# One PSUM ring for small products and staging, five result banks, and an earlier split of v

## The chip, the cores and the metric

The kernel runs on one core of a Trainium2 chip. The metric is the device time of one execution in microseconds. The engines are TensorE (PE: products; PEld: weight loads), VectorE (DVE), ScalarE (ACT), GpSimd (POOL), and SyncE (SP), which issues most of the transfers.

## The reference

One layer of a streaming encoder, 1024 positions by 1024 channels, in float32:

```
proj = x @ w_in + b_in                      # 4096 columns: u, h, c, b, gate_a, gate_b
y_a  = s5_ssm(u)                            # 32 groups of 16 channels, 64 complex states each
g    = gelu(y_a);  y_a = (g * sigmoid(g @ glu_w + glu_b)) @ w_ssm_out
z    = causal_conv3(c * h);  y_b = (b * z) @ w_conv_out      # v = b * z
x    = LayerNorm(alpha * x + (sigmoid(gate_a) * y_a + sigmoid(gate_b) * y_b) @ w_o)
x    = LayerNorm(alpha * x + (silu(x @ w_gate) * (x @ w_up)) @ w_down)
```

## The kernel before, in words

Every float32 operand of a large product is split into a high half (fp32r) and a low half, and each product is made of three: low by high, high by low, high by high (lines 183 to 185). The input projection and the feed-forward products work on pairs of column blocks with a scheme of seven products in place of eight (`Pair`, ORD_A): each of the seven steps of a pair forms a sum of weight blocks on POOL (`do_add`), splits it on ACT and DVE (`do_split`), and makes twelve products into one of the pair's four PSUM banks. The epilogues (`ev`) copy banks to SBUF on ACT, add them on POOL and DVE, and apply bias, sigmoid or convolution.

PSUM has eight banks of 2 KB in each partition, and one tile of 128 by 512 floats fills a bank. A pool is opened for a stage with `psum_open`: result banks have the tag "mm", n of them. In `psplit` a split stages its high half in PSUM (tag "hp"): ACT copies the raw block to the staging tile (line 137) and to the weights (line 138), and DVE subtracts the staging tile from the raw block (line 115), which frees the staging tile. The convolution stages in such tiles too (`conv`). The SSM branch makes four groups of small products for each of its eight chunks of channels: the transposes pst, the kernel pk, the states psw, the outputs psy, each of 128 by 512 floats at most. These take tiles of the tag "sm" (`small`). Within a tag, a tile takes the buffer that was allotted longest ago and waits for that buffer's last reader. From step 21 of the projection on, the pool psA has four banks for results, two for staging and two for small products.

All engines execute in order. The order is written out by a loop, `run`: at step s it issues the sum for step s+4 (POOL), the split for step s+3 (ACT, DVE), then one piece of each background generator (`bg`: the branch's `mats`, `rot`, `flow`, `gelu`, the convolution), then the twelve products of step s (PE), then epilogues that were put off by one step (`flush`), then the copies of step s. So a small product stands on PE ahead of the products of the step at which its generator is advanced. `begin_b` stands behind the last step of the projection (`steps[n_co - 1].mid`): it splits v into vh and vl, eight tiles, which the first products with w_conv_out (`pso`, the next steps) read. `begin_glu` closes psA.

Of the kernel before, what the change touches and what calls it, by code (L numbers as in the profile page):

```python
# [9 lines left out]
F32 = mybir.dt.float32  # L10
# [5 lines left out]
P = 128  # L16
# [31 lines left out]
def kernel(  # L48
# [29 lines left out]
    def opened(name, side="left", **kw):  # L78
        cm = pool(name, side, **kw)
        return cm, cm.__enter__()  # L80

    def close(cm):
        cm.__exit__(None, None, None)
# [33 lines left out]
    def ts(o, a, s1, s2, op0, op1, eng=V):  # L117
        eng.tensor_scalar(o, a, s1, s2, op0, op1)  # L118
# [7 lines left out]

    def staging(dt=F32):
        psum_state["k"] += 1
        return psum_state["p"].tile([P, 512], dt, tag="hp", name=f"hp{psum_state['k']}", bufs=2)

    def psplit(hi, lo, raw):
        if not psum_state["hp"]:
            return split(hi, lo, raw)
        hp = staging(F32R)
        if len(raw.shape) == 3:
            hp = hp.rearrange("p (a b) -> p a b", a=raw.shape[1])
        S.activation(hp, raw, AF.Copy)  # L137
        S.activation(hi, raw, AF.Copy)  # L138
        sub(lo, raw, hp.bitcast(F32))

    psum_state = {"k": 0, "hp": False}

    def psum_open(nm, n=8, hp=False):
        if "cm" in psum_state:
            close(psum_state["cm"])
        psum_state["cm"], psum_state["p"] = opened(nm, space=PSUM)
        psum_state["n"], psum_state["hp"] = n, hp

    def bank(nm):
        return psum_state["p"].tile([P, 512], F32, tag="mm", name=nm, bufs=psum_state["n"])  # L150
# [10 lines left out]
    class Step:  # L161
        load = add = split = mm = None

        def __init__(self):
            self.pre = []
            self.mid = []
            self.after = []

    class Entry:
        def __init__(self, nm):  # L170
# [132 lines left out]
    steps = []  # L303
# [15 lines left out]
    bg = []  # L319

    def flush():
        todo, later[:] = later[:], []
        for f in todo:
            f()

    def run(lo, hi):
        for s in range(lo, hi):
            for f in steps[s].pre:
                f()
            if s + 4 < len(steps) and steps[s + 4].add:  # L330
                steps[s + 4].add()
            if s + 3 < len(steps) and steps[s + 3].split:
                steps[s + 3].split()
            for it in list(bg):
                if it[1] <= s:
                    try:
                        it[1] = s + max(1, next(it[0]) or 1)
                    except StopIteration:
                        bg.remove(it)
            steps[s].mm()  # L340
            flush()
            for f in steps[s].mid + steps[s].after:
                f()
# [40 lines left out]
    def conv(p):  # L384
        q, z, cv = p.f, p.z, p.hs
        zf = z.rearrange("p b k -> p (b k)")
        V.memset(z[:, 0:2, 0:1], 0.0)
        V.tensor_copy(z[:, 0:2, 1:P], z[:, 8:10, 0:127])
        for h in range(2):
            hp = staging()  # L390
            o = 512 * h
            S.activation(hp, zf[:, 256 + o : 768 + o], AF.Copy, scale=cws[:, q, 2:3])
            V.scalar_tensor_tensor(hp, zf[:, 128 + o : 640 + o], cws[:, q, 1:2], hp, ALU.mult, ALU.add)
            V.scalar_tensor_tensor(cv[:, half(h)], zf[:, o : 512 + o], cws[:, q, 0:1], hp, ALU.mult, ALU.add)
            yield 1
        zt[q] = cv
# [36 lines left out]
    def make_x():  # L433
        waiting = []

        def low(h, l, k, src):
            (psplit if k % 2 else split)(h[:, k], l[:, k], src)

        for n, m in enumerate((4, 3, 1, 6, 7, 5, 2)):
            op = XOP[m]  # L440
            if len(op) == 3:
                sums = xcp.tile([P, 4, 512], F32, tag=("xh2", "xl2")[n % 2], name=f"xs{m}")
            h = xh[m] = xcp.tile([P, 4, 512], F32R, tag=f"xh{m}", name=f"xh{m}")
            l = xl[m] = xcp.tile([P, 4, 512], F32R, tag=f"xl{m}", name=f"xl{m}")
            for k in range(4):
                if len(op) == 1:
                    src = xr[op[0]][:, k]
                else:
                    src = sums[:, k]
                    tt(src, xr[op[1]][:, k], xr[op[2]][:, k], OPS[op[0]], G)  # L450
                waiting.append((h, l, k, src))
                if len(waiting) > 2:
                    low(*waiting.pop(0))
                yield 1
        for w in waiting:
            low(*w)
            yield 1
# [40 lines left out]
    def setup():  # L498
# [13 lines left out]
        def carve(*shape, at=None):  # L512
            n = int(np.prod(shape))
            o = used[0] if at is None else at
            if at is None:
                used[0] += n
            t = scr[:, o : o + n]
            return t.rearrange("p (a b) -> p a b", a=shape[0]) if len(shape) == 2 else t
# [10 lines left out]
        dt, a = carve(NG), carve(NG)  # L529
        m, r, q = carve(NG), carve(NG), carve(NG)  # L530
        th, hh, hl = carve(NG), carve(NG), carve(NG)
        it = carve(NG).bitcast(I32)
# [101 lines left out]
        for j in range(8):  # L634
            V.tensor_scalar_mul(sMim[:, :, j], x8[:, :, 7 - j], sgn[:, 0:1])
        ts(nLre, nLre, sgn[:, 0:1], -1.0, ALU.mult, ALU.mult)
        while psum_state["n"] > 4 or next(xg, None):
            yield 1
        close(xst_cm)
        open_ssm()  # L640
# [8 lines left out]
    st = [dict() for _ in range(8)]  # L649

    def small(nm):
        return psum_state["p"].tile([P, 4, P], F32, tag="sm", name=nm, bufs=2)

    def load_bc(cc):
        gs = slice(4 * cc, 4 * cc + 4)
# [4 lines left out]
    def mats(cc):  # L660
# [24 lines left out]
        if cc < 7:  # L685
            load_bc(cc + 1)
        yield 2
        ps = small(f"pst{cc}")
        for g in range(4):
            PE.transpose(ps[:, g, :], B[:, g].rearrange("p j c -> p (j c)"), ident)  # L690
        Bp = s["bp"] = stile([P, 4, P], "bp", f"bp{cc}")
        S.activation(Bp, ps, AF.Copy)
        yield 1
        pk = small(f"pk{cc}")
        for g in range(4):
            PE.matmul(pk[0:16, g, :], B[:, g, 7, :], Cp[:, g, 0:8, :].rearrange("p n c -> p (n c)"),
# [54 lines left out]
    def flow(cc):  # L751
        s = st[cc]
        yield 1
        while cc and "scan" not in st[cc - 1]:
            yield 1
        ps = small(f"psw{cc}")
        for g in range(4):
            PE.matmul(ps[:, g, :], s["bp"][:, g], s["UT"][:, g], start=True, stop=True)
# [217 lines left out]
    def begin_glu():  # L976
        while bg:
            spin()
        close(vst["cm"])
        psum_open("psB")  # L980
        cst_["wcm"], cst_["wp"] = opened("wp", "right")
        cst_["wo"] = []
# [19 lines left out]
    n_co = len(steps)  # L1002
    us = []
    gates = []
    for part in (1, None, 0):
# [8 lines left out]
        for d in range(8):  # L1014
# [3 lines left out]
            if d == 1:  # L1018
                steps.insert(-1, s_.pop(0))
            steps.extend(s_)  # L1020
    steps[n_co - 1].mid.append(begin_b)
    for k in (2, 3):
        steps[n_co - 12 + k].pre.append(lambda k=k: load_v(k))
    steps[n_glu].pre.append(begin_glu)
# [179 lines left out]
    def begin_d():  # L1204
        tr_x1(7, staging)
        close(cst_["tcm"])
        cst_["bcm"], cst_["bp"] = opened("xb")
        for f in make_x1(5):
            f()
# [34 lines left out]
    for f in range(NF):  # L1244
        p = Pair(wgu[0, f], wgu[1, f], f"f{f}", xcombo, epi_f)
# [10 lines left out]
    def begin_d0():  # L1256
        flush()
        psum_open("psD", 6, True)
        close(cst_["wcm"])
        cst_["zcm"], cst_["zp"] = opened("zp", "right")  # L1260
        load_z(0)
# [78 lines left out]


    psum_open("ps0", 6, True)
    pre_cm, pre = opened("pre")
    xst_cm, xst = opened("xst")
    sp = xst

    ramp = tb["ramp"] = pre.tile([P, P], F32, tag="ramp", name="ramp")
    dss = tb["dss"] = pre.tile([16, NG], F32, tag="dss", name="dss")
    early_setup = setup()
    next(early_setup)  # L1350
    raw = pairs[0].raw[1] = wring.tile([P, KT, P], F32, tag="raw", name="raw_u0_1", bufs=4)
# [36 lines left out]
    xg = make_x()  # L1388
# [9 lines left out]
                bg.remove(it)  # L1398

    def small_psum():  # L1400
        psum_open("psA", 4, True)

    steps[21].pre.append(lambda: (flush(), small_psum()))
    run(0, n_x)
    run(n_x, n_end - 1)
    last_after = steps[n_end - 1].after
    steps[n_end - 1].after = []
    run(n_end - 1, n_end)
    steps[n_end - 1].after = last_after

# [285 lines left out]
```

## Time and profile before

| | us |
|---|---|
| three timed runs | 1275.71, 3102.09, 6867.57 |
| their median | 3102.09 |
| the profiled execution | 1276.85 |
| its span, first to last instruction | 1275.1 |

The page gives the busy time of each engine over the span; the table by stretches gives it for any part. Of PE's waits the time-ordered list shows the idle time just before an instruction and what ended it, in square brackets.

### The profile page before, as it was taken

To read this page: it belongs to the slowest core of one execution; us is meant where nothing else is said; L and a number is where in the kernel's file an instruction comes from. 1 tells how busy PE (TensorE), PEld (TensorE's weight loads), DVE (VectorE), ACT (ScalarE), POOL (GpSimd) and SP (SyncE) were. 2 spreads that over 40 slices of the span, in tenths; PEclk is the share of its full clock that TensorE was granted. 3 is DMA by queue.
4 is the path that set the end of the run, shared out by engine and by line. 5 is a ranking of instruction groups with operands and counts; after the bars stand their busy time and mean duration, and the time that the engine had idled before them with its cause. 6 is when DMAs were issued, how large, how long until landed. Compare 5 with 4: busy or idle time off the path is not lost. (4 is left out here: it accounts for less than half of the span.)

```text
span 1275.1 us, 16761 instructions
## 1 busy us (share of the span) xinstructions
PE 1207.8 (95%) x5341; PEld 976.8 (77%) x5341; DVE 836.1 (66%) x1338; ACT 765.7 (60%) x1360; POOL 787.9 (62%) x593
## 2 busy tenths in 40 slices
PE   8769999999899999999979999999999999999996
PEld 4457787787677888888867888888888887888776
DVE  6986887979665656688875444444444447667777
ACT  4675777696876233133664555554555554778891
POOL 5747787797762214323488787777777764544466
PEclk9889999999998999999989999999999999999998
DMA  7122234344446544324303523233223417936312
GB/s 270 59 75 87 85 123 118 112 130 148 138 142 213 194 156 162 116 83 149 132 34 113 181 103 108 93 114 116 100 90 108 156 67 266 370 99 214 101 46 87
DMA packets 88455, 167.63 MB, mean 131 GB/s; under 512 B 17840, under 2 KB 27056, under 8 KB 88112
## 3 DMA queue, kind: packets, MB, share of 16 engines
q1 hardware_dynamic: 87760, 166.44, 39.1%
q8 instruction: 42, 0.69, 0.2%
q14 instruction: 45, 0.37, 0.1%
q10 hardware_dynamic: 608, 0.13, 0.1%
HBM read 116.34 MB, written 44.83 MB: 126 GB/s over the span
## 5 line engine op out<-in xcount | busy, mean ns | idle before, releaser
L183 PE MATMUL ps_f<-x1h,wl_f 128*128 128x512 f32 x616 | 241.7, 392 | 8.7 <-ACT keep L246 3.9
L184 PE MATMUL ps_f<-x1l,wh_f 128*128 128x512 f32 x616 | 240.8, 391 | 0.6 <-DVE x1l L115 0.6
L185 PE MATMUL ps_f<-x1h,wh_f 128*128 128x512 f32 x616 | 240.5, 390 | 0.0
L115 DVE TENSOR_TENSOR wl_f<-t_f,hp 128x512 fp32r<-128x512 f32 x107 | 73.5, 687 | 165.9 <-ACT hp L137 165.7
L137 ACT ACTIVATE hp<-t_f 128x512 fp32r<-128x512 f32 x107 | 64.4, 602 | 164.6 <-POOL t_f L106 158.3
L183 PEld LDWEIGHTS ps_f<-x1h,wl_f 128*128 128x128 f32 x616 | 116.2, 189 | 35.7 <-ACT keep L246 4.3
L184 PEld LDWEIGHTS ps_f<-x1l,wh_f 128*128 128x128 f32 x616 | 116.2, 189 | 24.9 <-DVE x1l L115 1.0
L185 PEld LDWEIGHTS ps_f<-x1h,wh_f 128*128 128x128 f32 x616 | 116.2, 189 | 24.2
L106 POOL TENSOR_TENSOR tB<-B,B 128x512 f32<-128x512 f32 x55 | 71.2, 1294 | 86.1 <-DVE rBl L115 45.4
L1517 PE MATMUL pe<-rBh,rAl 128*128 128x512 f32 x297 | 116.1, 391 | 3.5 <-DVE acc L1507 1.6
L1518 PE MATMUL pe<-rBl,rAh 128*128 128x512 f32 x297 | 115.8, 390 | 1.1 <-DVE rBl L115 1.1
L1519 PE MATMUL pe<-rBh,rAh 128*128 128x512 f32 x297 | 115.6, 389 | 0.0
L183 PE MATMUL ps_gt<-xh,wl_gt 128*128 128x512 f32 x216 | 89.3, 413 | 19.1 <-ACT ec_gt L237 6.2
L185 PE MATMUL ps_gt<-xh,wh_gt 128*128 128x512 f32 x216 | 87.3, 404 | 0.0
L184 PE MATMUL ps_gt<-xl,wh_gt 128*128 128x512 f32 x216 | 86.7, 401 | 0.0
L106 POOL TENSOR_TENSOR t_f<-raw_f,raw_f 128x512 f32<-128x512 f32 x63 | 81.7, 1297 | 2.2 <-DVE wl_f L115 2.0
L1517 PEld LDWEIGHTS pe<-rBh,rAl 128*128 128x128 f32 x297 | 55.7, 188 | 17.1 <-DVE acc L1507 2.5
L183 PEld LDWEIGHTS ps_gt<-xh,wl_gt 128*128 128x128 f32 x216 | 42.1, 195 | 32.0 <-issue 7.1
L138 ACT ACTIVATE wh_f<-t_f 128x512 fp32r<-128x512 f32 x107 | 66.0, 617 | 0.0
L1518 PEld LDWEIGHTS pe<-rBl,rAh 128*128 128x128 f32 x297 | 55.8, 188 | 13.3 <-DVE rBl L115 1.8
L1519 PEld LDWEIGHTS pe<-rBh,rAh 128*128 128x128 f32 x297 | 55.8, 188 | 11.6
L106 POOL TENSOR_TENSOR t_f<-raw_f 128x512 f32<-128x512 f32 x43 | 56.5, 1323 | 10.2 <-DMA raw_f<-in_wgu 9.5
(410 smaller groups left out, 3247.7 us busy)
## 6 DMA issues: line engine op xcount, KB each, us to landing
raw_f<-in_wgu SPq DMA_DIRECT2D x45, 512.0 KB, 4.0
As<-a_d SPq DMA_DIRECT2D x77, 256.0 KB, 3.7
a_d<-hs SPq DMA_DIRECT2D x55, 256.0 KB, 2.0
B<-in_wd SPq DMA_DIRECT2D x44, 256.0 KB, 5.3
s_d<-sg SPq DMA_DIRECT2D x32, 256.0 KB, 2.8
sgd<-s_d SPq DMA_DIRECT2D x16, 512.0 KB, 3.4
raw_gt<-in_w SPq DMA_DIRECT2D x15, 512.0 KB, 4.6
a_d<-hid SPq DMA_DIRECT2D x22, 256.0 KB, 2.1
```

The costliest lines, as they stand in the source:

```text
L106: eng.tensor_tensor(o, a, b, op)
L115: eng.tensor_tensor(o, a, b, ALU.subtract)
L137: S.activation(hp, raw, AF.Copy)
L138: S.activation(hi, raw, AF.Copy)
L183: PE.matmul(ps, self.lo[:, k, :], xh[:, k, :], start=first and k == 0, stop=False, skip_group_check=True)
L184: PE.matmul(ps, self.hi[:, k, :], xl[:, k, :], start=False, stop=False, skip_group_check=True)
L185: PE.matmul(ps, self.hi[:, k, :], xh[:, k, :], start=False, stop=last and k == 3, skip_group_check=True)
L1517: PE.matmul(ps, al[:, c], bh, start=kp == 0, stop=False)
L1518: PE.matmul(ps, ah[:, c], bl, start=False, stop=False)
L1519: PE.matmul(ps, ah[:, c], bh, start=False, stop=kp == NK - 1)
```

## The change

The tag "sm" goes. `small` allots from the tag "hp" like the staging, in a ring of 8 - n buffers; psA is opened with n = 5, so it has five result banks and a ring of three for staging and small products. The pools ps0 and psD have n = 6 and a staging ring of two as before. And `begin_b` is called through a new hook, `next`, directly behind the products of the projection's last step: ahead of the generators' pieces and of the put-off epilogues of that step, which in that one step are issued behind it.

```diff
     def staging(dt=F32):
         psum_state["k"] += 1
-        return psum_state["p"].tile([P, 512], dt, tag="hp", name=f"hp{psum_state['k']}", bufs=2)
+        return psum_state["p"].tile([P, 512], dt, tag="hp", name=f"hp{psum_state['k']}",
+                                    bufs=psum_state["hp"])
...
-        psum_state["n"], psum_state["hp"] = n, hp
+        psum_state["n"], psum_state["hp"] = n, 8 - n if hp else 0
...
+    def advance(s):
+        for it in list(bg):
+            if it[1] <= s:
+                try:
+                    it[1] = s + max(1, next(it[0]) or 1)
+                except StopIteration:
+                    bg.remove(it)
+
     def run(lo, hi):
...
-            for it in list(bg):
-                if it[1] <= s:
-                    try:
-                        it[1] = s + max(1, next(it[0]) or 1)
-                    except StopIteration:
-                        bg.remove(it)
-            steps[s].mm()
+            if steps[s].next:
+                steps[s].mm()
+                steps[s].next()
+                advance(s)
+            else:
+                advance(s)
+                steps[s].mm()
             flush()
...
-        while psum_state["n"] > 4 or next(xg, None):
+        while psum_state["n"] > 5 or next(xg, None):
...
     def small(nm):
-        return psum_state["p"].tile([P, 4, P], F32, tag="sm", name=nm, bufs=2)
+        return psum_state["p"].tile([P, 512], F32, tag="hp", name=nm, bufs=psum_state["hp"]).rearrange(
+            "p (g k) -> p g k", g=4)
...
-    steps[n_co - 1].mid.append(begin_b)
+    steps[n_co - 1].next = begin_b
...
     def small_psum():
-        psum_open("psA", 4, True)
+        psum_open("psA", 5, True)
```

On ACT, at the end of the projection, the order before is this (gy is the gelu, sg the sigmoid of a gate, vh the high half of v):

```order
L121 ACTIVATE wh_so_1_0_3787<-raw_so_1_3679 128x512
L817 ACTIVATE gy_0_3715<-gy_0_3715 128x512
L817 ACTIVATE gy_1_3717<-gy_1_3717 128x512
L407 ACTIVATE sg_0_0_3821<-eb_gt_3704,b1s 128x512
L121 ACTIVATE vh<-vr_z 128x512
L121 ACTIVATE vh<-vr_ws 128x512
```

And this is it with the change (the lines are 10 or 11 higher there):

```order
L121 ACTIVATE wh_so_1_0_3787<-raw_so_1_3679 128x512
L828 ACTIVATE gy_0_3715<-gy_0_3715 128x512
L828 ACTIVATE gy_1_3717<-gy_1_3717 128x512
L121 ACTIVATE vh<-vr_z 128x512
L121 ACTIVATE vh<-vr_ws 128x512
```

The sigmoid moved behind the eight copies of v, and its store on SP with it; the two gelu instructions did not move. On PE, DVE and POOL no instruction changes its place.

Where the ring is used, the order stays, and what changes is which tile has a buffer before which. On ACT, at the branch's first chunk, hp36 to hp39 are staging tiles, bp0 is the copy out of the transposes pst0, K0 the copy out of pk0:

```order
L137 ACTIVATE hp36_920<-t_hc0_6_882 128x512
L138 ACTIVATE wh_hc0_6_918<-t_hc0_6_882 128x512
L137 ACTIVATE hp37_946<-t_hc1_2_916 128x512
L138 ACTIVATE wh_hc1_2_944<-t_hc1_2_916 128x512
L372 ACTIVATE hs0_940<-ps_hc0_1_866,b1s_70 128x512
L137 ACTIVATE hp38_968<-t_hc1_5_942 128x512
L138 ACTIVATE wh_hc1_5_966<-t_hc1_5_942 128x512
L692 ACTIVATE bp0_977<-pst0_972 128x512
L137 ACTIVATE hp39_996<-t_hc1_1_964 128x512
L138 ACTIVATE wh_hc1_1_994<-t_hc1_1_964 128x512
L699 ACTIVATE K0_1005<-pk0_1000 16x512
```

In the ring of three the tiles come as hp36, hp37, hp38, pst0, hp39, pk0: pst0 takes the buffer of hp36 and waits for that split's low half, and pk0 that of hp38.

## Rows read from the trace of the kernel before

**Rows 1.** The page: the span; busy us of an engine, share, instructions.

```profile
span 1275.1 us, 16761 instructions
...
PE 1207.8 (95%) x5341; PEld 976.8 (77%) x5341; DVE 836.1 (66%) x1338; ACT 765.7 (60%) x1360; POOL 787.9 (62%) x593
```

**Rows 2.** Stretches: their length, each engine's busy us, granted clock, DMA share, GB/s.

```profile
99.00:388.00 289.00, 273.94 (x1310) 222.08 (x1309) 224.34 (x315) 216.81 (x368) 222.48 (x159) 0.99 0.41 125
388.00:404.00 16.00, 16.00 (x71) 13.12 (x71) 4.14 (x7) 8.68 (x16) 3.85 (x3) 1.00 0.76 253
404.00:414.00 10.00, 7.06 (x18) 5.01 (x17) 8.36 (x14) 7.86 (x15) 0.00 (x0) 0.66 0.35 103
```

**Rows 3.** PE in order of time: start, us, instruction [idle before <-releaser]; bank waits.

```profile
120.97 0.50 PE L183 MATMUL ps_hc<-xh,wl_hc 128*128 128x512 f32 x1 [0.25 <-DVE ec_hc L112]
...
239.29 0.50 PE L183 MATMUL ps_gt<-xh,wl_gt 128*128 128x512 f32 x1 [2.18 <-DVE ec_hc L112]
...
240.71 0.63 PE L184 MATMUL ps_gt<-xl,wh_gt 128*128 128x512 f32 x1
```

**Rows 4.** ACT and PE in order of time, around the split of v.

```profile
406.35 0.72 ACT L407 ACTIVATE sg<-eb_gt,b1s 128x512 f32<-128x512 f32 x1
406.97 0.61 ACT L121 ACTIVATE vh<-vr_z 128x512 fp32r<-128x512 f32 x1
...
407.64 0.80 PE L183 MATMUL pso<-vh,wl_so 128*128 128x512 f32 x1 [2.94 <-ACT vh L121]
```

**Rows 5.** Waits of ACT, 99 to 388 us: total us, times, longest.

```profile
ACT hp L137 <- DVE zE L387: 4.7, 2, 3.7
...
ACT hp L392 <- DVE hs L394: 1.2, 1, 1.2
...
ACT eb_hc L234 <- PE ps_hc L185: 1.0, 1, 1.0
```

**Rows 6.** PE in order of time, the first, third and last of seven waits.

```profile
309.53 1.03 PE L696 MATMUL pk<-cp,bst 128*16 128x128 f32 x8 [1.53 <-DVE cp L115]
...
336.65 1.03 PE L696 MATMUL pk<-cp,bst 128*16 128x128 f32 x8 [2.48 <-DVE cp L115]
...
372.39 0.50 PE L183 MATMUL ps_gt<-xh,wl_gt 128*128 128x512 f32 x1 [0.86 <-ACT ea_gt L231]
```

**Rows 7.** PE and DVE in order of time: small products, splits ahead in the ring.

```profile
113.41 0.60 PE L690 MATMUL pst<-ident,bst 128*128 128x128 f32 x4
113.73 0.69 DVE L115 TENSOR_TENSOR wl_hc<-t_hc,hp 128x512 fp32r<-128x512 f32 x1 [1.82 <-ACT hp L137]
...
258.15 1.05 PE L758 MATMUL psw<-ut,bp 128*128 128x128 f32 x8
263.29 0.68 DVE L115 TENSOR_TENSOR wl_b<-t_b,hp 128x512 fp32r<-128x512 f32 x1
...
383.51 0.38 PE L789 MATMUL psy<-ut,T 128*128 128x128 f32 x2
383.45 0.68 DVE L115 TENSOR_TENSOR wl_gt<-t_gt,hp 128x512 fp32r<-128x512 f32 x1
```

**Rows 8.** PE and ACT in order of time: last products, the copies of them.

```profile
121.13 0.58 ACT L692 ACTIVATE bp<-pst 128x512 f32<-128x512 f32 x1
...
172.74 0.39 PE L185 MATMUL ps_b<-xh,wh_b 128*128 128x512 f32 x1
174.65 0.58 ACT L234 ACTIVATE eb_b<-ps_b 128x512 f32<-128x512 f32 x1
...
243.50 0.39 PE L185 MATMUL ps_gt<-xh,wh_gt 128*128 128x512 f32 x1
243.93 0.60 ACT L231 ACTIVATE ea_gt<-ps_gt 128x512 f32<-128x512 f32 x1
...
288.84 0.39 PE L185 MATMUL ps_gt<-xh,wh_gt 128*128 128x512 f32 x1
290.04 0.58 ACT L231 ACTIVATE ea_gt<-ps_gt 128x512 f32<-128x512 f32 x1
```

More of the change, by code (lines that the diff above doesn't have):

```diff
@@ L139, in psplit @@
         sub(lo, raw, hp.bitcast(F32))
-    psum_state = {"k": 0, "hp": False}
+    psum_state = {"k": 0, "hp": 0}
     def psum_open(nm, n=8, hp=False):
@@ L167, in __init__ @@
             self.after = []
+            self.next = None
     class Entry:
```

## The prediction

> **What bounds the kernel now.** I read the page first, then the stretch the change touches, then its waits. TensorE is busy for 1207.8 of the 1275.1 us of the span [rows 1], so the whole kernel can give back 67 us at most, and the change touches only the stretch from 99 to some 454 us: there the PSUM pool psA is open, which holds the result banks, the staging of the splits and the small products of the SSM branch. The table by stretches [rows 2] shows that this stretch is no plain TensorE stretch. From 99 to 388 us PE is busy for 273.9 of 289 us, POOL for 222.5 (77%), DVE for 224.3 and ACT for 216.8. From 404 to 414 us PE stands at 7.1 of 10 us, with a granted clock of 0.66.
>
> Two sorts of PE wait are what the change aims at. The first is the wait for a result bank: five of them, the first of 0.25 and the last of 2.18 us, together 6.0 us [rows 3]. Each is the first product into a bank that the pair before has not given back, and the releaser is the DVE step that reads that bank. The second is the 2.94 us before the first product with v [rows 4].
>
> What the reader is to see next is who is late there. In the list of waits of ACT from 99 to 388 us, ACT waits for PE once, for 1.0 us [rows 5]; neither DVE nor POOL appears with a wait for PE in theirs. POOL, ACT and DVE wait for each other, and PE runs between them: its results are ready some microseconds before ACT takes them, its weights are ready a little before it needs them. The waits of PE from 309.53 to 372.39 us, seven of them with 8.0 us in all (1.53 the first, 0.86 the last), are of the kind that five banks don't touch: a matrix of the branch that DVE has not finished, or a bank of the same pair that ACT has still to copy [rows 6].
>
> **The change part by part.**
>
> *Five result banks.* The five bank waits go: 6.0 us off PE's own time up to 239 us. But what PE gains there it loses again by 372.39 us: the seven waits of [rows 6] are for work of the other engines, which by [rows 5] does not hang on PE's being early. So I count this part at 0. The ends are -6.0 us (all of it stays) and 0.
>
> *One ring of three for staging and small products.* Nothing is added or removed on an engine; the instructions of PE, DVE and POOL keep their order. What moves is what a small product waits for. Before, it took one of two banks of its own, free for a long time. Now it takes the slot of the third tile before it in the ring, mostly a staging tile of a split, and that one is given back when DVE has made the low half. The splits stand three steps ahead in the program, so a small product on PE, in order ahead of the step's twelve products, now waits for a split that only a later step needs. The price by the rows of before: the first group of four transposes starts at 113.41 and its slot is free at 113.73 + 0.69 = 114.42, so it is 1.0 us late; a later group starts at 258.15 and its slot is free at 263.29 + 0.68 = 263.97, which is 5.8 us, the largest; the last starts at 383.51 against 383.45 + 0.68 = 384.13, 0.6 us [rows 7]. Read off in this way, 29 of the 32 small groups are late, by 0.6 to 5.8 us, 3.2 us on average and 92 us in sum.
>
> They don't add up as long as the other engines keep their times: once PE has waited 5 us it stands 5 us later against POOL, ACT and DVE, and the next small group finds its slot free. The sum of these waits is then a single shift of PE, 5.8 us at most, and the 8.0 us of waits in [rows 6] swallow it before the stretch ends. So the new waits cost 0 at the lower end, and 92 us, where everything shifts with PE each time, at the upper one; a third slot can also help ACT (below), so the term's own lower end is -5.9 us.
>
> I take a value near the lower end, by the lead that PE has over ACT. It is 121.13 - 114.01 = 7.1 us at the first chunk, but not so everywhere. ACT takes a result at 174.65 us which PE ended at 172.74 + 0.39 = 173.13, a lead of 1.5 us; at 243.93 against 243.50 + 0.39 = 243.89 none; at 290.04 against 288.84 + 0.39 = 289.23, 0.8 us [rows 8]. A PE that is 4.5 us late (my choice, half way between the mean of 3.2 and the largest of 5.8) makes ACT late there by 3.0, 4.5 and 3.7 us, 11.2 us together. Against that stand waits of ACT itself for a staging slot that the third slot relaxes: 4.7 us in two waits for hp and 1.2 us in one more [rows 5] (the longest took 3.7 us). That is 5.9 us back. The term is 11.2 - 5.9 = +5.3 us. After 388 us PE is the bound again (16.0 of 16 us busy [rows 2]), so what is left there reaches the end in full.
>
> *v split directly behind the last product.* On ACT the sigmoid of the last pair's first result (0.72 us at 406.35) now stands behind the eight copies of v and not ahead; the copies start at 406.97, so they move up by 0.62 us, and PE waits for the first of them [rows 4]. The two instructions of the gelu ahead of them stay where they are, because the branch's generator has nothing to issue in that last step; that is why only 0.6 of the 2.94 us goes. What is late next is the gelu itself. The sigmoid's store to DRAM starts about 5 us later on SP, and its reader comes many steps after; I price that at 0. Should the shorter wait also spare the low clock behind it, there is more: 0.66 over 10 us is 6.8 us at the lower level (1.2 GHz), worth 3.4 us at most [rows 2]. I don't count on it, since PE waited 2.18 us at 239.29 [rows 3] and its products, 0.39 us each at 2.4 GHz, took 0.63 us behind that wait too.
>
> **The sum.** The profiled execution took 1276.85 us. 1276.85 + 0 (banks) + 5.3 (ring) - 0.6 (v) = 1281.6, so **1282 us**. The median of the three runs shown, 3102.09 us, is no measure of this program: one run took 1275.71, within 0.1% of the profiled one, and nothing in the profile would fill the other two. My numbers are for an execution like the profiled one.
>
> **The rivals.**
>
> *It gains* (1264 us). All 6.0 us of bank waits and the 5.9 us of ACT's waits for staging are won, and PE's new waits stay inside what it had to spare: 1276.85 - 6.0 - 5.9 - 0.6 = 1264.4. For it: the bank waits are real and end on DVE, and ACT never waits for PE. Against it: the waits after 309 us would have to shrink too. The Trainium skill says this in "Perfetto Trace Analysis", section "Optimizing Tensor Performance", Matmuls: independent groups should rotate through different PSUM banks, so that the evacuation of one overlaps the next one's products. By that rule alone the result would be this rival's; the trace shows the wait that the rule speaks of, with 6.0 us, and shows beside it that the products behind wait for something else.
>
> *Slower, by waits that add up* (1312 us). In the middle of the stretch, from the third to the sixth chunk of the branch, PE's lead over ACT is about 1 to 4 us, and less at two places [rows 8]. If a PE late by 4 us makes ACT, and through it POOL and the next split, late by as much, the next small product meets the same wait again. Of the 92 us, 36 belong to the ten late groups between 175 and 275 us, the 5.8 us of [rows 7] among them: 1276.85 + 36 - 0.6 = 1312. For it speak those leads; against it, that POOL has 23% of the stretch free [rows 2] and can catch up while PE waits. It decides the time where PE's lateness passes ACT's lead at every chunk; with the whole stretch rigid it would be 1276.85 + 92 = 1369.
>
> *Slower, by the clock* (1303 us). Each new wait of some 3 us may be followed by matmuls at half speed. If one per chunk did, at up to 3.4 us, eight would cost 27: 1276.85 + 27 - 0.6 = 1303. For it: the wait of 2.18 us at 239.29 did [rows 3]. Against it: the mean clock from 99 to 388 is 0.99 with the twelve waits of [rows 3, 6] in it [rows 2], and a PE that is slowed in this stretch meets its next wait later. The Trainium skill has such a case in "TensorE: Matmul & The Clock Gate", section "A second HAM failure mode: psum-queue depth-cycling": a kernel that cycles through PSUM banks idles between groups so often that the clock swings between its two levels. It speaks against this change; here the waits that it would need appear only in the changed kernel.
>
> *Nothing but v* (1276 us). PE's shift is swallowed wholly by the 8.0 us of [rows 6]; only the 0.6 us remain.
>
> **How the numbers follow.** My forecast of 1282, with 1277 to 1293 for a ring term from 1 us to one and a half times the 11.2, has 0.52; the gain 0.23; nothing but v 0.11; waits that add up 0.10; the clock 0.04. The range for 8 in 10 runs from 1266 to 1300: it leaves out most of the two slower rivals and the far end of the gain. Two per cent, about what a measurement of this kernel can tell from no change, are 1251 and 1302. Faster by more would need over 25 us, where PE has about 15 us of waits to give from 99 to 388 and 3 behind: 0.01. Slower by more is the rival of waits that add up and part of the clock's: 0.11. The rest, 0.88, is within.
>
> **What would show it.** Right: no PE wait left that ends on a DVE read of another pair's bank; in their place waits of PE before pst, pk and psw that end on DVE's low halves, large at the first chunk and then small; the wait before the first product with v at about 2.3 us; the last product of the projection some 5 us later. Wrong: small products that wait 3 us at every chunk (the waits add up), POOL or ACT with waits for PE all along, a mean clock below 0.97 from 99 to 388, or a stretch that ends before 400 us.

## The result and the profile after

The changed kernel takes 1285.02 us in the median of five runs (lowest 1281.63), the kernel before 1277.85 us beside it (lowest 1275.71). The ratio is 1.0061 [1.0047, 1.0075]: slower by 0.6%, about 7.8 us. Runs that a disturbance stretched (3102 and 6868 us before, 1510 us after) are in these two medians, but not in the ratio nor in anything that follows. The profiled execution took 1286.7 us, the longest of the other four.

The page of the changed kernel, its span and the busy time of PE, against [rows 1]:

```profile
span 1284.9 us, 16718 instructions
...
PE 1212.3 (94%) x5341; PEld 980.7 (76%) x5341; DVE 831.2 (65%) x1338; ACT 768.5 (60%) x1360; POOL 783.4 (61%) x593
```

PE makes the same 5341 products and is busy 4.5 us longer; the span is 9.8 us longer. All of that arises in one stretch. From the first product of the pair under way at 99 us to the end of the projection's last product the kernel before takes 305.25 us (99.45 to 404.70), the changed one 315.01 (99.92 to 414.93). From the first product with v to the end both take the same: 1275.1 - 407.64 = 867.5 and 1284.9 - 418.06 = 866.8 us.

Three windows of that stretch show two losses. The columns are those of [rows 2], with the length ahead of the comma. The kernel before:

```profile
99.00:250.00 151.00, 143.97 (x679) 116.06 (x678) 119.43 (x175) 106.36 (x185) 120.13 (x88) 0.99 0.36 108
250.00:310.00 60.00, 58.47 (x290) 48.23 (x289) 51.39 (x70) 48.84 (x80) 48.67 (x34) 1.00 0.46 141
310.00:404.00 94.00, 87.51 (x416) 70.91 (x414) 57.66 (x79) 70.28 (x118) 57.54 (x42) 1.00 0.52 166
```

The changed kernel:

```profile
99.00:250.00 151.00, 140.06 (x663) 113.93 (x662) 116.58 (x173) 106.91 (x184) 114.72 (x85) 0.99 0.36 105
250.00:310.00 60.00, 54.25 (x261) 43.90 (x260) 45.45 (x69) 45.08 (x74) 42.67 (x32) 0.94 0.45 139
310.00:404.00 94.00, 88.83 (x418) 72.25 (x416) 61.01 (x79) 71.05 (x117) 63.37 (x46) 0.96 0.47 145
```

First, PE idles more: 305 us less the busy times is 15.1 us before and 21.9 after. Second, the granted clock falls. A window at 0.94 has spent 6 in 50 of its time at the lower level (1.2 GHz), 7.2 us of 60; by all three that is 3.0 us before and 3.0 + 7.2 + 7.5 = 17.7 after. The shares are rounded; the trace's clock record itself has 3.9 and 17.1 us in the stretch.

The waits of PE from 99 to 404 us in the changed kernel, all ten groups of them (total us, times, longest), answer to [rows 3, 6]:

```profile
PE pk L707 <- DVE zE L397: 5.3, 1, 5.3
PE pk L707 <- ACT bp L703: 4.1, 2, 3.1
PE pk L707 <- DVE wl_hc L115: 3.7, 1, 3.7
PE psy L800 <- DVE hs L404: 2.0, 1, 2.0
PE psw L769 <- DVE wl_gt L115: 1.9, 1, 1.9
PE pst L701 <- DVE wl_hc L115: 1.6, 1, 1.6
PE pk L707 <- DVE wl_b L115: 1.2, 1, 1.2
PE psy L800 <- DVE wl_gt L115: 1.0, 1, 1.0
PE pk L707 <- DVE wl_gt L115: 0.6, 1, 0.6
PE psw L769 <- DVE wl_b L115: 0.5, 1, 0.5
```

Every wait of the kernel before is gone, the five for banks among them. In their place stand eleven, 21.8 us in sum, and every one is before a group of small products. Each ends on the reader of an older tile of the ring: the low half of a split (L115), the convolution's read of its staging tile (L404), or ACT's copy of pst (L703). The first line is one of L115 too, as the rows below show, so the splits have 15.7 of the 21.8 us. The two waits for the copy of pst (3.14 and 0.98 us, in the seventh and eighth chunk) show that a tile does not always take the buffer that was allotted longest ago: one split's tile is allotted between pst and pk, and pk took pst's buffer, two tiles back and not three.

Now the longest of them, PE and DVE in order of time (start, us, instruction, count, idle before with its releaser):

```profile
250.10 0.40 PE L187 MATMUL ps_gt<-xh,wh_gt 128*128 128x512 f32 x1
...
255.02 0.68 DVE L115 TENSOR_TENSOR wl_gt<-raw_gt,hp 128x512 fp32r<-128x512 f32 x1
...
255.65 0.06 DVE L397 MEMSET zE<- 128x2 f32 x1
255.75 1.89 PE L707 MATMUL pk<-cp,bst 128*16 128x128 f32 x8 [5.25 <-DVE zE L397]
...
257.57 0.80 PE L185 MATMUL ps_gt<-xh,wl_gt 128*128 128x512 f32 x1
...
258.16 0.63 PE L186 MATMUL ps_gt<-xl,wh_gt 128*128 128x512 f32 x1
...
259.87 0.47 PE L187 MATMUL ps_gt<-xh,wh_gt 128*128 128x512 f32 x1
260.18 0.40 PE L185 MATMUL ps_gt<-xh,wl_gt 128*128 128x512 f32 x1
```

The view names L397, but that is a memset of zE, which pk neither reads nor overwrites; it ends at 255.71, 0.01 us behind the low half of a split (255.02 + 0.68 = 255.70), on the same engine. In the program pk waits for that low half. Eight products of pk took 1.03 us in [rows 6] and take 1.89 here; the products behind them take 0.63 and not 0.39 until 260. The trace's clock record has 1.2 GHz from 253.2 to 260.0, that is from within the wait. The same follows the waits of 3.67 us (to 122.49; low from 123.5 to 126.9) and 3.14 us (to 322.65; low from 321.5 to 328.3).

The waits of ACT from 99 to 388 us, which held PE once with 1.0 us [rows 5]:

```profile
ACT K L710 <- PE pk L707: 4.5, 1, 4.5
...
ACT ec_gt L239 <- PE ps_gt L187: 3.8, 4, 1.6
ACT ea_gt L233 <- PE ps_gt L187: 3.6, 2, 2.1
...
ACT eb_hc L236 <- PE ps_hc L187: 1.6, 2, 1.1
```

All sixteen lines of this kind together are some 24 us. So PE's lateness does reach ACT, as [rows 8] let one fear. ACT's waits for a staging tile that DVE still reads fell from 7.9 us to 2.7. And the place around v, ACT and PE in order of time, against [rows 4]:

```profile
412.95 0.64 ACT L824 ACTIVATE gl<-gy 128x512 f32<-128x512 f32 x1 [2.53 <-DMA gy<-y_d]
...
416.25 1.24 ACT L828 ACTIVATE gy<-gy 128x512 f32<-128x512 f32 x2 [1.57 <-DVE gl L827]
417.39 0.62 ACT L121 ACTIVATE vh<-vr_z 128x512 fp32r<-128x512 f32 x1
...
418.06 0.80 PE L185 MATMUL pso<-vh,wl_so 128*128 128x512 f32 x1 [3.13 <-ACT vh L121]
```

The sigmoid is out of the way: the copy follows the gelu by 1.14 us, where it was 406.97 - 405.20 = 1.77. But the gelu, held by the load of gy, starts 1.32 us behind PE's last product (414.93) and not 0.50 (404.70). The wait before v is 3.13 us, 0.2 longer than before.

### The profile page after: what moved, and what is told of

Same layout as the page of the kernel before. It is cut to its first block, busy times and chain, and to the rows that moved or that the text cites. A ratio compares the mean times of both kernels' runs of the same rounds, so it can differ in the third digit from the quotient of the medians.

```text
span 1284.9 us, 16718 instructions
## 1 busy us (share of the span) xinstructions
PE 1212.3 (94%) x5341; PEld 980.7 (76%) x5341; DVE 831.2 (65%) x1338; ACT 768.5 (60%) x1360; POOL 783.4 (61%) x593
## 5 line engine op out<-in xcount | busy, mean ns | idle before, releaser
L115 DVE TENSOR_TENSOR wl_f<-t_f,hp 128x512 fp32r<-128x512 f32 x107 | 73.5, 687 | 166.1 <-ACT hp L138 165.8
L185 PE MATMUL ps_gt<-xh,wl_gt 128*128 128x512 f32 x216 | 89.0, 412 | 10.7 <-DVE scr L112 6.1
L106 POOL TENSOR_TENSOR t_f<-raw_f 128x512 f32<-128x512 f32 x43 | 56.6, 1326 | 10.2 <-DMA raw_f<-in_wgu 9.6
L109 POOL TENSOR_TENSOR hid<-sgf,ec_f 128x512 f32<-128x512 f32 x21 | 27.5, 1311 | 54.0 <-DVE sgf L109 29.1
```

The lines of the kernel that those rows point to most:

```text
L106: eng.tensor_tensor(o, a, b, op)
L109: eng.tensor_tensor(o, a, b, ALU.mult)
L115: eng.tensor_tensor(o, a, b, ALU.subtract)
L185: PE.matmul(ps, self.lo[:, k, :], xh[:, k, :], start=first and k == 0, stop=False, skip_group_check=True)
```

## The experiments

Thirteen runs, each against the kernel before on the same chip, with the 95% interval of the ratio. The stretch is taken as above, from the profiled execution (first ps_hc product after 98 us to the end of the last ps_gt product); the time at 1.2 GHz is that of the clock record within it. These columns are of one execution each, and not always a middling one: those of e3 to e6 are the fastest of theirs, those of the changed kernel and of e2 are the slowest of theirs, and those of e8, e8 again and e10 the slowest but one. The last column is the granted clock from the first to the last instruction, as a mean over all executions of the row. In e4, e7 and e10 the stretch begins behind a bank wait of 1.5 to 1.8 us that it leaves out (they begin at 101.2 to 102.2 us, the others at 98.8 to 100.2).

| kernel | ratio [interval] | stretch, us | PE idle in it | at 1.2 GHz | wait before v | mean clock |
|---|---|---|---|---|---|---|
| before | 1 | 305.25 | 15.1 | 3.9 | 2.94 | 0.983 |
| changed | 1.0061 [1.0047, 1.0075] | 315.01 | 21.9 | 17.1 | 3.13 | 0.979 |
| e1: v alone | 0.9985 [0.9977, 0.9994] | 305.28 | 14.0 | 6.8 | 2.33 | 0.984 |
| e2: changed, without v | 1.0061 [1.0045, 1.0076] | 315.91 | 21.9 | 20.9 | 2.94 | 0.978 |
| e3: small products behind | 1.0002 [0.9994, 1.0011] | 305.49 | 14.9 | 4.2 | 2.58 | 0.982 |
| e4: 4 banks, ring of 4 | 0.9977 [0.9967, 0.9986] | 301.43 | 13.3 | 0 | 2.14 | 0.983 |
| e5: 6 banks, ring of 2 | 1.0145 [1.0130, 1.0159] | 324.51 | 29.0 | 20.5 | 2.15 | 0.976 |
| e6: 5 banks, 2 staging, 1 small | 1.0043 [1.0030, 1.0055] | 311.70 | 18.9 | 17.1 | 2.20 | 0.978 |
| e7: e4 and e3 together | 1.0003 [0.9992, 1.0013] | 303.08 | 11.9 | 6.8 | 2.10 | 0.982 |
| e8: 4 banks, ring of 3 | 1.0068 [1.0052, 1.0084] | 317.46 | 23.3 | 20.5 | 2.94 | 0.978 |
| e8 again | 1.0065 [1.0049, 1.0081] | 315.93 | 19.8 | 21.1 | 2.36 | 0.978 |
| e9: e8, three waits filled | 1.0052 [1.0033, 1.0072] | 312.24 | 12.5 | 3.5 | 1.42 | 0.982 |
| e9 again | 1.0042 [1.0030, 1.0055] | 312.22 | 12.5 | 3.7 | 1.45 | 0.982 |
| e10: e4 without v | 0.9990 [0.9981, 0.9999] | 303.63 | 10.7 | 13.7 | 3.49 | 0.982 |
| e11: e8, nine waits filled | 1.0014 [1.0005, 1.0023] | 309.98 | 5.5 | 0 | 1.62 | 0.985 |

### Which part costs: e1 and e2

v alone (the kernel before with the hook):

```diff
-    steps[n_co - 1].mid.append(begin_b)
+    steps[n_co - 1].next = begin_b
```

> The kernel before with nothing but v split directly behind the projection's last product; four result banks, two staging tiles and two small ones as before. Theory (the prediction's): the copies of v move up by one sigmoid, 0.6 us of PE's 2.94 us go, ratio to before 0.9995. Rival (the copies hang on the gelu that stands ahead of them on ACT and on its load from DRAM): PE's wait keeps 2.8 to 3.2 us and the ratio is 1.000. If moving v were what costs, it would be above 1.002.

Measured 0.9985, about 1.9 us, three times the 0.6 that the shorter wait gives. The wait is 0.61 us shorter, and PE's row shows what else:

```profile
407.49 0.50 PE L184 MATMUL pso<-vh,wl_so 128*128 128x512 f32 x1 [2.33 <-ACT vh L121]
...
408.55 0.40 PE L186 MATMUL pso<-vh,wh_so 128*128 128x512 f32 x1
```

The products behind the wait run at 0.40 us. From 404 to 414 us the clock is 1.00, where [rows 2] has 0.66. Over all executions the mean clock is 0.9838 against 0.9830 for the kernel before beside it; 0.0008 of 1276 us is 1.0 us, so the wait and the clock make about 1.6 of the 1.9 us.

The ring alone (the changed kernel with the line put back):

> The changed kernel with v split where it was before; five result banks and the ring of three stay. Theory (the ring costs): ratio to before 1.005 to 1.008, PE's waits before small products from 99 us to the end of the projection still 18 to 25 us. Rival (the move of v costs, by what it delays): at most 1.002.

Measured 1.0061, the same as with v. So the ring and the banks carry the loss, and v gives nothing that two such intervals can show in their company: there its wait is as long as before (3.13 and 2.94 us). The six executions of e2 also show the clock's part without a trace: they run from 1280.05 us with a mean clock of 0.983 to 1287.51 us with 0.976.

### How the ring is met: e3 and e4

In e3 a step's pieces of the branch are issued behind its twelve products, not ahead:

```diff
             else:
-                advance(s)
                 steps[s].mm()
+                advance(s)
```

> The changed kernel, with every piece of the background generators issued behind the twelve products of its step and not ahead of them; on PE alone the order changes, each small product stands one step's products (2.75 us) later. Theory (a small product stands on PE ahead of products that could run while its slot comes free): PE's waits before small products fall from 21.8 to under 8 us, the half-clock stretches between 99 and 400 us from three to at most one, ratio to before 0.995 to 1.001. Rival (the shared ring holds up the staging, so ACT and DVE are late whatever PE does): the ratio stays at 1.004 to 1.008.

The time is back at the kernel before, 1.0002, with the low clock down to 4.2 us (3.9 before). PE still waits 11.1 us before small groups, more than expected, but in pieces of 2.1 us at most. In e4 the fifth bank goes to the ring:

```diff
-        psum_open("psA", 5, True)
+        psum_open("psA", 4, True)
```

> The changed kernel with four result banks as before and a ring of four for staging and small products. Theory (a slot of three back comes free too late): with the slot four back the waits before small products fall from 21.8 to under 8 us, the 6 us of bank waits come back, ratio 0.999 to 1.002. Rival (sharing as such costs, and five banks give back part of it): 1.006 to 1.012.

Measured 0.9977 [0.9967, 0.9986], 2.9 us faster than the kernel before: the lowest ratio of all (the intervals of e1 and e10 overlap its own). Of its PE waits from 99 to 404 us the three longest groups and one for a bank:

```profile
PE pk L707 <- DVE wl_gt L115: 4.5, 3, 2.6
PE psy L800 <- ACT wh_gt L139: 3.2, 1, 3.2
PE ps_hc L185 <- DVE eb_gt L112: 1.5, 1, 1.5
PE psy L800 <- DVE wl_hc L115: 1.4, 1, 1.4
```

Small groups wait 11.5 us, where less than 8 was expected; the gain came all the same. The clock is 1.00 in all three windows of the profiled execution, the fastest of ten; the mean over all ten is 0.983, as before, so in the mean e4 does not gain by the clock.

### Which buffers matter: e5, e6, e8 and e7

Each is the changed kernel with other numbers. e5 has six result banks and a ring of two (`psum_open("psA", 6, True)`, with the pool known by its name where the set-up waits for it):

> The changed kernel with six result banks and a ring of two for staging and small products. Theory (PE's waits before small products grow as the ring gets shorter, and the low clock behind them with it): with the slot two back PE waits for the last split but one; waits before small products 35 to 80 us after 21.8 with three, ratio to before 1.015 to 1.04. Rival (the waits are a single shift of PE that later waits swallow, whatever the ring): 1.004 to 1.010.

1.0145, just under the expected range; PE waits 29.0 us before small products, and 35 to 80 were expected. That is more than with a ring of three, so the rival fell. e6 shares nothing: staging has two buffers, small products have one of their own.

```diff
-        return psum_state["p"].tile([P, 512], F32, tag="hp", name=nm, bufs=psum_state["hp"]).rearrange(
+        return psum_state["p"].tile([P, 512], F32, tag="sm", name=nm, bufs=1).rearrange(
...
+        psum_state["hp"] = 2
```

> The changed kernel with five result banks, two staging tiles of their own and one tile for the small products, so nothing is shared. Theory (what costs is when the slot comes free, not that it is shared): pk now waits for ACT's copy of pst, which in the kernel before ended 3.0 to 5.5 us after pk's start in six of the eight chunks; waits before small products 12 to 25 us, ratio to before 1.002 to 1.007. Rival (sharing the ring with the staging is what costs, and five banks pay without it): 0.995 to 0.999.

1.0043: the small products now wait for ACT to read the small group before them, 18.4 us in sum, and the cost is 0.0043 in place of 0.0061. So a slot that comes free late costs without any sharing. e8 takes the fifth result bank away and leaves it unused:

```diff
-        psum_open("psA", 5, True)
+        psum_open("psA", 4, True)
+        psum_state["hp"] = 3
```

> The changed kernel with four result banks and the ring of three; one bank of PSUM stays unused. It prices the fifth bank. Theory (what PE gains at the banks it loses at later waits, so the fifth bank is worth at most 2 us): ratio to before 1.004 to 1.008, like the changed kernel's 1.0061. Rival (the fifth bank gives back its 6 us of waits in the changed kernel): 1.010 to 1.012.

1.0068, and 1.0065 when run again beside later kernels (

> The kernel with four result banks and the ring of three once more, on the same chip as the filled one: 1.0068 within 0.0015 by both theories.

), against 1.0061: the fifth bank is worth 0.0004 to 0.0007, or 0.5 to 0.9 us, and the intervals of about 0.0015 to either side overlap. The rival's 1.010 to 1.012 lies outside them. e7 joins the ring of four with e3's order:

> The changed kernel with four result banks, a ring of four and the generators' pieces issued behind the products of their step. Theory: PE's waits before small products fall from the 11.5 us of the ring of four to under 5 us, and the time to 0.995 to 0.998 of before. Rival (the ring of four leaves only waits that the other engines' pace sets, and PE has to wait for that pace somewhere): the same as the ring of four alone, 0.9977 within 0.001.

Both fell: 1.0003. The small groups wait only 4.0 us, as expected, but PE waits 9.2 us elsewhere (2.6 for copies by ACT, 2.1 and 1.5 for banks among them), and the clock fell three times for 3.4 us, once of them behind v (407.8 to 411.2 us). Why PE's other waits grow when its small groups wait less was not settled.

### The clock or the waits: e9 and e11

These keep the waits and the tile order of e8, but give PE unread products into the eighth bank during them; they add work and leave nothing out. e9 puts 14, 20 and 13 ahead of the pk of chunks 0, 4 and 6 (10.8 us):

```diff
+        if cc in FILL:
+            fb = psum_state["p"].tile([P, 512], F32, tag="fill", name=f"fill{cc}", bufs=1)
+            for _ in range(FILL[cc]):
+                PE.matmul(fb, xh[2][:, 0, 0:P], xh[2][:, 0, :], start=True, stop=True)
```

> Four result banks and the ring of three, and in the eighth bank products that nobody reads: 14, 20 and 13 of them on PE ahead of the small products pk of the chunks 0, 4 and 6, whose waits are 3.7, 5.3 and 3.5 us without them. At 0.23 us each they are 10.8 us of PE work more, put into waits. Theory (the lower clock behind these three waits costs as much as a wait): the half-clock stretches at 121, 254 and 323 us go, and in spite of the added work the time falls by 4 to 6 us against the same kernel without them: ratio to before 1.002 to 1.004. Rival (what PE loses at half clock it would wait for anyway): 1.006 to 1.008. If the fill costs its own time: above 1.010.

The three falls of the clock are gone from the profile (the clock is 0.99, 1.00 and 1.00 in the three windows; a new one of 3.4 us stands at 233.2). The profiled execution took 1280.99 us, against 1287.16 and 1285.05 in the two profiles of e8. The ratio moved less: on the same chip 1.0052, where e8 has 1.0065, between what the two theories expected, and e9's runs lie far apart (1277.09 to 1286.16). It was run again:

> The kernel with three waits filled once more: 1.0052 within 0.002; by the clock theory between the one with all waits filled and the unfilled one's 1.0066, by the rival equal to both.

1.0042, again between the two ranges. That is a gain of 0.0013 to 0.0026 on e8, with intervals as wide as that: not enough by itself to tell the two theories apart. So e11 fills nine waits, with 76 products and 17.4 us:

```diff
+    FILL = {'pst0': 5, 'pk0': 14, 'psw1': 7, 'pk2': 4, 'psy2': 7, 'pk4': 20, 'pk6': 13, 'pk7': 3, 'psy6': 3}
+
     def small(nm):
+        if nm in FILL:
+            fb = psum_state["p"].tile([P, 512], F32, tag="fill", name=f"fill_{nm}", bufs=1)
+            for _ in range(FILL[nm]):
+                PE.matmul(fb, xh[2][:, 0, 0:P], xh[2][:, 0, :], start=True, stop=True)
```

> Four result banks and the ring of three, with products that nobody reads ahead of nine small groups (5 before pst0, 14, 20, 13, 4, 3 before pk0, pk4, pk6, pk2, pk7, 7 before psw1, 7 and 3 before psy2 and psy6): 76 of them, 17.4 us at 0.23 us each, in place of nearly all of PE's 20 to 23 us of waits. Theory (about half of the loss is PE at half clock behind the waits): no half-clock stretch from 105 us to the end of the projection in the profile, ratio to before 1.001 to 1.004. Rival (waiting alone is the loss, since PE must wait for the others' pace anyway): 1.006 to 1.009.

Measured 1.0014 [1.0005, 1.0023], and its runs lie within about 4 us. The windows of e11:

```profile
99.00:250.00 151.00, 148.13 (x705) 120.42 (x704) 116.57 (x174) 106.72 (x184) 116.60 (x87) 1.00 0.36 106
250.00:310.00 60.00, 58.69 (x288) 48.05 (x288) 46.16 (x68) 47.70 (x78) 44.56 (x32) 1.00 0.45 139
310.00:404.00 94.00, 92.65 (x446) 75.83 (x446) 60.52 (x80) 70.49 (x119) 61.42 (x45) 1.00 0.51 157
```

Those of e8, without the filling:

```profile
99.00:250.00 151.00, 138.93 (x655) 112.64 (x654) 114.91 (x170) 105.94 (x183) 113.17 (x85) 0.98 0.35 103
250.00:310.00 60.00, 54.20 (x259) 43.85 (x259) 45.19 (x69) 44.41 (x75) 41.59 (x31) 0.94 0.45 140
310.00:404.00 94.00, 88.53 (x416) 71.98 (x415) 61.83 (x81) 71.58 (x119) 63.55 (x46) 0.96 0.47 144
```

And PE around the longest wait in e11, in order of time:

```profile
248.68 0.40 PE L187 MATMUL ps_gt<-xh,wh_gt 128*128 128x512 f32 x1
248.91 4.71 PE L667 MATMUL fill_pk<-xh 128*128 128x512 f32 x20
254.40 1.05 PE L713 MATMUL pk<-cp,bst 128*16 128x128 f32 x8 [0.78 <-DVE zE L397]
255.37 0.50 PE L185 MATMUL ps_gt<-xh,wl_gt 128*128 128x512 f32 x1
255.71 0.39 PE L186 MATMUL ps_gt<-xl,wh_gt 128*128 128x512 f32 x1
```

The useful products stand still as long as in e8 (248.91 to 254.40 us is 5.5 us; all told 5.5 + 17.4 = 22.9 us in e11, 23.3 and 19.8 in the two profiles of e8), but behind them pk takes 1.05 us and the products 0.39. The stretch is 7.5 us shorter (6.0 by e8's second profile) and the ratio 0.0051 to 0.0054 lower, some 6.6 us: useless work made the kernel faster. In the stretch that is more than half of e8's loss, 7.5 of 12.2 us, or 6.0 of 10.7; the profiled executions differ by 9.3 us, of which 2.4 arise behind it, by a shorter wait before v and 3.4 us less at 1.2 GHz there.

### What a ring of four gives without v: e10

> Four result banks and the ring of four with v split where it was before. Theory (the move of v gives 0.0015, by keeping the clock, and the ring of four what is left of the 0.0023): 0.9990 to 0.9996. Rival (all of the gain is the ring's): 0.9977.

0.9990, at the edge of what was expected; so of e4's 0.0023 the ring of four gives 0.0010 and v 0.0013. The two intervals overlap, so the halves are known to about 0.001 only; the rival, 0.9977, lies just outside e10's interval. The mean clocks, 0.9831 in e4 and 0.9818 in e10, differ by 1.7 us in 1275, which is what v is credited with.

## Why the prediction was right and wrong

- **The direction and the place: right.** Slower by less than 2%, by the ring, from 99 us to the end of the projection, and not behind it. Forecast 1282, ratio 1.0040 to the profiled execution; measured 1.0061.
- **Five banks, 0: right.** The five bank waits went and bought next to nothing; by e8 the part is 0.5 to 0.9 us, with intervals that leave out the 6.0. The Trainium skill's rule on rotating through PSUM banks ("Perfetto Trace Analysis", section "Optimizing Tensor Performance", Matmuls) agrees with the trace on the wait: 6.0 us of it vanished here. The time did not follow, because what decided was whom the products behind wait for.
- **The ring, +5.3: right in kind and near in size, in part by luck.** Small products wait for a split that only a later step needs, and the largest wait is 5.25 us (5.8 at most was forecast). But two steps of the working were wrong. The waits were to be a single shift of PE, 5.8 us at most, which the old waits swallow: there are eleven, 21.8 us in sum, in place of 15.1, and the projection's last product ends 10.2 us later (414.93 against 404.70), not 5. The sign "large at the first chunk and then small" was wrong with it: pk waits 5.25 us in the fifth chunk and 3.14 in the seventh. And ACT was to wait 11.2 us for PE; it waits some 24. What the ring costs with the clock kept up is e11's stretch: 309.98 - 305.25 = +4.7 us. (The kernel before has 3.9 us at 1.2 GHz in its stretch, at most 1.8 us of loss that e11 has not; counted so, it is 4.7 to 6.5.) That this lies at the 5.3 owes something to the chosen 4.5 us.
- **The clock, priced at 0 in the sum and 0.04 as a rival: the failed step.** The ring with the clock falling is +9.8 us in the stretch (changed), +12.2 and +10.7 (e8), where e11 has +4.7. So what was missing in the sum is 5.0 to 7.5 us of half-speed products. The mean clock of all executions says the same: 0.979 for the changed kernel and 0.978 for e2 and e8, where the kernel before has 0.983; 0.004 to 0.005 of 1276 us is 5 to 6 us. I had weighed the wait of 2.18 us in [rows 3] against a mean of 0.99, and not that the new waits would be longer than those of before in that stretch. The rival was wrong in its count, eight falls; there are three, each behind a wait of over 3 us. The place agrees in part with the Trainium skill's "TensorE: Matmul & The Clock Gate", section "A second HAM failure mode: psum-queue depth-cycling": idle gaps between groups, and a clock between two levels (0.94 and 0.96 in two windows). In this trace the falls stand behind the three longest gaps, and behind none of the eight of 2.0 us and less. The mean from 99 to 388 us is 0.969 (17.7 us of 289 at 1.2 GHz), just past the 0.97 that I had set as a sign against me.
- **v, -0.6: right as a step, wrong as a gain here.** The copies moved up by 0.63 us behind the gelu, as said. Alone (e1) that gave 0.61 us and kept the clock behind it, together 1.9, the part I had put aside. In the changed kernel the gelu itself came 0.8 us later against PE (its load of gy), which I had named as late next and given no price, and no gain shows.
- **Rivals.** The gain fell: it needed [rows 6] to shrink, and new waits came instead. "Nothing but v" fell. "Waits that add up" was right that lateness is met again (eleven waits, not one), but at 21.8 us in all, in place of the old 15.1. It forecast 1312, and its 36 us did not come.

**What stays open.** The reckoning by rows does not quite close: 6.8 us more idle, and 13.2 us more at half speed make 11, against 9.8: 3.7 of the 13.2 are wait, and the other 9.5, at 0.43 us a product in place of 0.23, lose 4.4. And e9 took the same three falls away for 0.0013 to 0.0026 (1.7 to 3.3 us), where the profiled executions differ by 4.1 to 6.2. Part of that is the clock: the profiled executions of e9 have 0.985, the other ten 0.982 in the mean, and 0.003 of 1281 us is 4 us. But in the second run of e9 the time does not follow the clock (1278.55 us at 0.981, 1281.02 at 0.985), so the rest stays open.

## What to carry to other kernels

Before tiles of two kinds share a ring, count on the order written out how many allotments back a tile's buffer lies and when that one's last reader ends: here a small product needed now got the buffer of a split needed three steps later, and depths of two, three and four gave 1.0145, 1.0068 and 0.9977 (e5, e8 and e4, all with v moved; e5 with six result banks, the others with four). Of a new wait on PE, price what follows it too, from a row at the lower clock. And to tell a wait's own cost from the clock's, fill the wait with unread products: if the kernel gets faster, it was the clock.

## What was not expected of the hardware

- Unread products of 17.4 us, put into waits, made a kernel some 6.6 us faster (e8 to e11).
- A wait's length alone did not tell whether the clock falls. The wait before v was 2.33 us in e1 and 2.14 in e4, with the clock at 1.00 behind it; 2.10 in e7, with 3.4 us at 1.2 GHz; 2.94 before and 3.13 in the changed kernel, with 6.8 us each; 3.49 in e10, with 3.4.
- At 1.2 GHz the products follow each other at 0.43 us and not 0.23 (258.16 to 258.59, and 260.18 to 260.41 in the changed kernel): a fall of 6.8 us loses at most 3.2 us, as [rows 2] had let one reckon.
